# Distance bias made inside the loop over x and moved to GpSimd's queue, first half's final norm among the second half's products, result stored by partition

## The chip, the cores and the metric

The kernel runs on one core of one Trainium2 chip. The metric is the device time of one execution in microseconds (us). Before the change it is 2591.85 us, the median of three runs (2590.37 to 2592.15).

A core has engines that each work through their own list of instructions in order: PE (TensorE, matrix products, results into eight PSUM banks of 128 x 512 f32), DVE (VectorE) and ACT (ScalarE) for elementwise work, POOL (GpSimd) and SP (SyncE). Transfers between the chip's memory (HBM) and the on-chip memory (SBUF) are issued here by SP and by POOL; each of the two feeds a queue of its own, and 16 DMA engines carry out both.

## The reference, cut to what matters

One decoder layer on 512 tokens of width 2048:

```python
u = rmsnorm(h, norm_mix_g)
qa, ka, va, qb, kb, vb, g_low, ob_gate, gate_a, gate_b = split(u @ w_in)
ya = sliding_window_attention(qa, ka, va, sinks, rel_bias) @ w_proj_a
yb = (rmsnorm(gated_linear_attention(qb, kb, vb, log_a)) * silu(ob_gate)) @ w_proj_b
h = h + (sigmoid(gate_a) * ya + sigmoid(gate_b) * yb) @ w_out
z = rmsnorm(h, norm_ffn_g)
h = h + (silu(z @ w_ffn_gate) * (z @ w_ffn_up)) @ w_ffn_down
return rmsnorm(h, norm_final_g)
```

In the attention (16 heads, 4 key heads, window 128) a score gets a bias that depends on the head and on the distance between query and key alone, looked up in `rel_bias` (32 buckets x 16 heads), and minus 1e30 outside the window.

## The kernel before, in words

Everything is laid out transposed: features on the 128 partitions, the 512 tokens along the free axis, so the 2048 features are 16 tiles (k or m, `KD` = 16). Each f32 operand is split into a high and a low part in the matmul's own format (`split`, L201: ACT casts the high part, DVE subtracts for the low part), and a product is three matmuls (`mm3`, L238, lines 240 to 242). Weights come in pieces of 128 x 1024 f32, 512 KB. `load_piece` (L212) issues the load of a piece on SP's queue at L219 and splits it; there are three buffers each for the raw piece, its high part and its low part, so SP issues the load of a piece only when the piece three places earlier has been split. `next_piece` (L226) loads ahead by two and also calls up to two closures from a list `side`, which holds work to be put among the products.

Outside of one block that is ordered by hand (the FFN), a planner orders each engine's instructions: by the place in the program where an instruction could run, by readiness in the planner's own reckoning otherwise. Each engine then keeps the planned order and waits where reality is later.

The first stage is the loop over x, L308 to L334: for each of the 16 tiles of x, `fetch` (L298) loads a tile and half a piece of the key and value weights, four tiles ahead. ACT and DVE make `uh` and `ul`, four PSUM banks collect keys and values (12 matmuls per k), and the squares are summed into `ssq`. Then come the first norm (L339: the sums over partitions by PE, the inverse root as a power on POOL at L264 in `inv_rms`, the spreading over partitions by PE in `across`, L273), and behind it the distance bias, L344 to L366: four small loads (`sink_b`, the one-hot table `oh`, `rbt` and the mask `outm`); one matmul pair that picks for each of 16 heads a row of 383 biases by distance (`ps_rb`, L353); one addition of the mask on DVE (`by_dist`); and one DMA that writes each head's row 128 times to memory (`bias_d`, 16 x 128 x 383 f32, 3064 KB). From there each head's 128 x 256 bias tile is read with a stride of one row less one element, which shifts each partition's row by one: L496, two loads of 256 KB for each of the four head groups, at the head of the loop over groups (L486), before the group's query products (`ps_qa`, four pieces, 96 matmuls). The scores of a group (L418, L419) and their masking with the bias on DVE (L424, `attention_weights`) are put into `side` and so come among the products of the group behind it.

The last stage is the last of the eleven down products, L1232 to L1260. It is done in two halves of 256 tokens. For each half, 16 products (12 matmuls of 256 columns each) are added into `acc` by DVE (L1241), squared by ACT (L1246), and the squares summed by DVE (L1248). Then `token_sums` (four matmuls, L283), `inv_rms` (DVE, then POOL), `across` (two diagonals on DVE, matmuls L273), a copy of the result by ACT (L1256), and six calls of `scale_out` (L1213), which scale 1, 1, 2, 4, 4 and 4 of the 16 tiles, on DVE (L1222) or POOL (L1220), and store them through SP (L1230). The six calls of half 0 are put into `side`, one of them after every odd m of half 1; those of half 1 come at the end. The result lies in memory as tile, partition, token, so a stored row is 256 f32 long, 1 KB.

Of the kernel before, what the change touches and what calls it, by code (L numbers as in the profile page):

```python
# [12 lines left out]
F32 = mybir.dt.float32  # L13
# [3 lines left out]
ALU = mybir.AluOpType  # L17
AX = mybir.AxisListType

P = 128  # L20
D = 2048
T = 512
KD = D // P
NT = T // P
A_HEADS, A_KV, HD = 16, 4, 64
WINDOW = 128
N_BUCKETS, MAX_DISTANCE = 32, 128
# [20 lines left out]
TLEN = 383  # L48
# [4 lines left out]
HALF = T // 2  # L53
# [75 lines left out]
def hybrid_layer(  # L129
# [37 lines left out]
    def slot(name, dtype=F32):  # L167
        return tpool.tile([P, T], dtype, tag="t", name=name)

    def work(name, dtype=F32):  # L170
        return held_by["work"].tile([P, T], dtype, tag="w", name=name)
# [4 lines left out]
    def aux_bank(name):  # L176
        pool = banks_of["aux"]
        return pool.tile([P, T], F32, tag="aux" if pool is psa else "mm", name=name)
# [78 lines left out]
    def inv_rms(ssq, n, name, cols=4):  # L257

        ms = small.tile([P, cols], F32, tag="ms", name=f"ms_{name}")
        nc.vector.tensor_scalar(  # L260
            out=ms, in0=ssq, scalar1=1.0 / n, scalar2=EPS, op0=ALU.mult, op1=ALU.add
        )
        r = small.tile([P, cols], F32, tag="rstd", name=f"rstd_{name}")
        nc.gpsimd.tensor_tensor(out=r, in0=ms, in1=halves[:, :cols], op=ALU.pow)  # L264
        return r
# [12 lines left out]
    def token_sums(sqs, name, cols=4):  # L278

        bank = aux_bank(f"ps_s_{name}")  # L280
        for tt in range(cols):
            for i, sq in enumerate(sqs):
                nc.tensor.matmul(  # L283
                    bank[:, tt : tt + 1],
                    lhsT=sq[:, tt * P : (tt + 1) * P],
                    rhs=ones[:, 0:1],
                    start=(i == 0),
                    stop=(i == len(sqs) - 1),
                )
        return bank[:, 0:cols]  # L290


    uh, ul = [], []
    ssq = slot("ssq")
    kv_banks = [mm_bank("ps_kv_0"), mm_bank("ps_kv_1"), aux_bank("ps_kv_2"), aux_bank("ps_kv_3")]
# [12 lines left out]
    for k in range(KD):  # L308
        if k + 4 < KD:
            fetch(k + 4)  # L310
        xt, wf, part = fetched[k]
        wh, wl = (t[:, part] for t in ahead[k // 2])
        uh.append(slot(f"uh_{k}", F32R))
        ul.append(slot(f"ul_{k}", F32R))
        gcol = g_mix_sb[:, k : k + 1]
        nc.scalar.activation(uh[k], xt, AF.Copy, scale=gcol)
        nc.vector.scalar_tensor_tensor(
            out=ul[k],
            in0=xt,
            scalar=gcol,  # L320
            in1=uh[k].bitcast(F32),
            op0=ALU.mult,
            op1=ALU.subtract,
        )
        split(wh, wl, wf[:, part])
        for m in range(4):
            cols = slice(m * P, (m + 1) * P)
            mm3(kv_banks[m], wh[:, cols], wl[:, cols], uh[k], ul[k], k == 0, k == KD - 1)
        if k == 0:
            nc.scalar.activation(ssq, xt, AF.Square)  # L330
        else:
            sq = work(f"xsq_{k}")
            nc.scalar.activation(sq, xt, AF.Square)
            nc.vector.tensor_tensor(out=ssq, in0=ssq, in1=sq, op=ALU.add)  # L334
    taken[0] = KD // 2
    for i in range(2):
        load_piece(taken[0] + i)
# [1 line left out]
    nc.vector.tensor_copy(rstd1, inv_rms(token_sums([ssq], "mix"), D, "mix"))  # L339
    rb1 = const.tile([P, T], F32, name="rb1")  # L340
    nc.vector.tensor_copy(rb1, across(rstd1, "mix"))


    sink_b = const.tile([P, A_HEADS], F32, name="sink_b")  # L344
    nc.sync.dma_start(sink_b, sinks.to_broadcast([P, A_HEADS]))
    oh = work("oh")
    nc.sync.dma_start(oh[0:N_BUCKETS, 0:TLEN], onehot)
    rbt = small.tile([N_BUCKETS, A_HEADS], F32, tag="rbt", name="rbt", bufs=1)
    nc.sync.dma_start(rbt, rel_bias)
    outm = work("outm")  # L350
    nc.sync.dma_start(outm[0:A_HEADS, 0:TLEN], outside)
    ps_rb = aux_bank("ps_rb")
    nc.tensor.matmul(  # L353
        ps_rb[0:A_HEADS, 0:TLEN], lhsT=rbt, rhs=oh[0:N_BUCKETS, 0:TLEN], start=True, stop=True
    )
    by_dist = work("by_dist")
    nc.vector.tensor_tensor(
        out=by_dist[0:A_HEADS, 0:TLEN],
        in0=ps_rb[0:A_HEADS, 0:TLEN],
        in1=outm[0:A_HEADS, 0:TLEN],  # L360
        op=ALU.add,
    )
    nc.sync.dma_start(
        bias_d,
        by_dist[0:A_HEADS, 0:TLEN].rearrange("h (o t) -> h o t", o=1).to_broadcast([A_HEADS, P, TLEN]),
    )  # L366

    kh, kl = [], []
    for m in range(2):
# [116 lines left out]
    for g in range(A_KV):  # L486
        bias = []
        for hp in range(2):
            b = slot(f"bias_{g}_{hp}").rearrange("p (h k) -> p h k", h=2)
            h0 = 4 * g + 2 * hp  # L490
            src = bass.AP(
                bias_d.tensor,
                bias_d.offset + h0 * P * TLEN + (P - 1),
                [[TLEN - 1, P], [P * TLEN, 2], [1, 2 * P]],
            )
            nc.sync.dma_start(b, src)  # L496
            bias.append(b)
        banks = project(uh, ul, f"qa{g}")
        qs = []
        for m in range(2):  # L500
            qf = slot(f"qf_{g}_{m}")
            nc.vector.tensor_tensor(out=qf, in0=banks[m], in1=rb1, op=ALU.mult)
            for half in range(2):
                rows = slice(half * HD, (half + 1) * HD)
                other = slice((1 - half) * HD, (2 - half) * HD)
                q = slot(f"q_{g}_{m}_{half}", F32R)
                nc.scalar.activation(q[rows], qf[rows], AF.Copy, scale=HD**-0.5)
                nc.vector.scalar_tensor_tensor(
                    out=q[other],
                    in0=qf[rows],  # L510
                    scalar=HD**-0.5,
                    in1=q[rows].bitcast(F32),
                    op0=ALU.mult,
                    op1=ALU.subtract,
                )
                qs.append(q)
        for n in range(NT):
            side.append(partial(attention_weights, g, n, qs, bias, held))
            if n:
                side.append(partial(attention_values, g, n - 1, held))  # L520
        side.append(partial(attention_values, g, NT - 1, held))
# [691 lines left out]
    def scale_out(m0, n, tag, cols, bank, rb):  # L1213

        out = wpool.tile([P, 4, HALF], F32, tag=tag, name=f"out_{cols.start}_{m0}")
        for i in range(n):
            m = m0 + i
            a = acc[m][:, cols]
            if by_gpsimd(m):
                nc.gpsimd.tensor_tensor(out=out[:, i], in0=a, in1=rb, op=ALU.mult)  # L1220
            else:
                nc.vector.scalar_tensor_tensor(  # L1222
                    out=out[:, i],
                    in0=a,
                    scalar=g_final_sb[:, m : m + 1],
                    in1=bank,
                    op0=ALU.mult,
                    op1=ALU.mult,
                )
        nc.sync.dma_start(outT[m0 : m0 + n, :, cols].rearrange("m p t -> p m t"), out[:, 0:n])  # L1230

    for half in range(2):  # L1232
        cols = slice(half * HALF, (half + 1) * HALF)
        sums = work(f"osum_{half}")[:, 0:HALF]
        for m in range(KD):
            wh, wl = wd[m]
            bank = mm_bank(f"ps_fd_{half}_{m}")[:, 0:HALF]
            for j in range(4):
                mm3(bank, wh[:, j], wl[:, j], fh[j][:, cols], fl[j][:, cols], j == 0, j == 3)
            a = acc[m][:, cols]  # L1240
            nc.vector.tensor_tensor(out=a, in0=bank, in1=a, op=ALU.add)  # L1241
            if m == 0:
                nc.scalar.activation(sums, a, AF.Square)
            else:
                s2 = work(f"osq_{half}_{m}")[:, 0:HALF]
                nc.scalar.activation(s2, a, AF.Square)  # L1246
            if 0 < m < KD - 1:
                nc.vector.tensor_tensor(out=sums, in0=sums, in1=s2, op=ALU.add)  # L1248
            if by_gpsimd(m):
                nc.scalar.activation(a, a, AF.Copy, scale=g_final_sb[:, m : m + 1])  # L1250
            if m % 2 == 1 and side:
                side.pop(0)()
        r = inv_rms(token_sums([sums, s2], f"fin{half}", 2), D, f"fin{half}", 2)
        bank = across(r, f"fin{half}", 2)[:, 0:HALF]
        rb3 = slot(f"rb3_{half}")[:, 0:HALF]
        nc.scalar.copy(rb3, bank)  # L1256
        m0 = 0
        for n, tag in zip((1, 1, 2, 4, 4, 4), ("wf", "wh", "wl") * 2):
            side.append(partial(scale_out, m0, n, tag, cols, bank, rb3))
            m0 += n  # L1260
    while side:
        side.pop(0)()

# [49 lines left out]
```

## Time and profile before

| | |
|---|---|
| median of 3 runs | 2591.85 us |
| the profiled execution | 2590.59 us, of which the span from the first to the last instruction or transfer is 2588.8 us |
| PE busy | 2545.2 us, 98% of the span |
| DVE, ACT, POOL busy | 1501.4, 1005.9 and 159.4 us |
| DMA | 415.05 MB, 160 GB/s over the span |
| queue of SP, of POOL | 371.15 MB (45.6% of the DMA engines' span), 41.95 MB (10.6%) |

In the rows below, a row of a timeline has start, duration, engine, line, operation, the tile written and those read, and the shapes. Matmuls are pipelined, and each is shown until its modelled end, so that rows overlap; the pace is read from the starts. "Waits" names who ended an idle time, with the sum, the number and the longest.

### The profile page before, as it was taken

To read this page: it belongs to the slowest core of one execution; us is meant where nothing else is said; L and a number is where in the kernel's file an instruction comes from. 1 tells how busy PE (TensorE), PEld (TensorE's weight loads), DVE (VectorE), ACT (ScalarE), POOL (GpSimd) and SP (SyncE) were. 2 spreads that over 40 slices of the span, in tenths; PEclk is the share of its full clock that TensorE was granted. 3 is DMA by queue.
4 is the path that set the end of the run, shared out by engine and by line. 5 is a ranking of instruction groups with operands and counts; after the bars stand their busy time and mean duration, and the time that the engine had idled before them with its cause. 6 is when DMAs were issued, how large, how long until landed. Compare 5 with 4: busy or idle time off the path is not lost.

```text
span 2588.8 us, 30598 instructions
## 1 busy us (share of the span) xinstructions
PE 2545.2 (98%) x11678; PEld 2109.2 (81%) x11678; DVE 1501.4 (58%) x2209; ACT 1005.9 (39%) x1436; POOL 159.4 (6%) x202
## 2 busy tenths in 40 slices
PE   8999999999999999999899999999999999999997
PEld 7777888888888888888688888888888888888886
DVE  6695463643333334446975766666666657575755
ACT  5464332322222223223444444444344444444443
POOL 0000000000000000000001011110111010101011
PEclk9999999999999999999999999999999999999998
DMA  6622223234333332544578787777878787878782
GB/s 197 130 80 65 90 74 98 74 122 128 124 123 110 96 97 65 197 144 144 198 208 207 209 202 221 198 213 187 234 186 225 198 219 203 213 204 209 207 216 101
DMA packets 151730, 415.05 MB, mean 160 GB/s; under 512 B 15888, under 2 KB 24256, under 8 KB 151584
## 3 DMA queue, kind: packets, MB, share of 16 engines
q1 hardware_dynamic: 128544, 371.15, 45.6%
q0 software_dynamic: 23040, 41.95, 10.6%
q8 instruction: 91, 1.49, 0.2%
q14 instruction: 55, 0.45, 0.1%
HBM read 355.38 MB, written 57.66 MB: 160 GB/s over the span
## 4 chain that ended last, share of the span: by engine, by line
PE 82%; issue 11%; DVE 5%; DMA 1%; ACT 1%; POOL 0%; SPq 0%; DVEq 0%; ACTq 0%; POOLq 0%
PE ps_ua L970 8%; PE ps_fd L241 6%; PE ps_fd L242 6%; PE ps_fd L240 6%; PE ps_ue L970 5%; PE ps_uf L970 5%; PE ps_ub L970 4%; PE ps_ud L970 4%; PE ps_uc L970 4%; PE ps_ga L240 2%; PE ps_ga L241 2%; PE ps_gb L240 2%; PE ps_gb L241 2%; PE ps_ga L242 2%; PE ps_gb L242 2%
## 5 line engine op out<-in xcount | busy, mean ns | idle before, releaser
L1168 DVE TENSOR_TENSOR tl<-wq,th 128x1024 fp32r<-128x1024 f32 x420 | 511.2, 1221 | 457.3 <-ACT th L1165 455.0
L1165 ACT CAST th<-wq 128x1024 fp32r<-128x1024 f32 x420 | 441.5, 1052 | 457.9 <-PE ps_ua L970 116.5
L204 DVE TENSOR_TENSOR wl<-wf,wh 128x1024 fp32r<-128x1024 f32 (+1 forms) x176 | 206.3, 1173 | 378.5 <-ACT wh L203 369.9
L203 ACT CAST wh<-wf 128x1024 fp32r<-128x1024 f32 (+1 forms) x176 | 177.9, 1012 | 536.4 <-PE ps_ga L241 115.7
L240 PE MATMUL ps_fd<-fh,th 128*128 128x512 f32 x640 | 249.1, 389 | 0.0
L241 PE MATMUL ps_fd<-fl,th 128*128 128x512 f32 x640 | 249.0, 389 | 0.0
L242 PE MATMUL ps_fd<-fh,tl 128*128 128x512 f32 x640 | 249.0, 389 | 0.0
L1116 POOL DMA_DIRECT2D h_d<-fd x160 | 138.3, 864 | 1154.1 <-ACT fd L1115 1148.4
L1115 ACT COPY fd<-ps_fd 128x512 f32<-128x512 f32 x160 | 93.9, 587 | 289.3 <-PE ps_fd L242 286.7
L240 PEld LDWEIGHTS ps_fd<-fh,th 128*128 128x128 f32 x640 | 120.1, 188 | 25.0
L241 PEld LDWEIGHTS ps_fd<-fl,th 128*128 128x128 f32 x640 | 120.1, 188 | 24.9
L242 PEld LDWEIGHTS ps_fd<-fh,tl 128*128 128x128 f32 x640 | 120.1, 188 | 24.9
L970 PE MATMUL ps_ue<-th,zs 128*128 128x512 f32 x352 | 123.7, 392 | 2.2 <-DVE c L1032 2.2
L240 PE MATMUL ps_wo<-mgh,th 128*128 128x512 f32 x256 | 99.8, 390 | 1.5 <-DVE sgb L805 1.2
L242 PE MATMUL ps_wo<-mgh,tl 128*128 128x512 f32 x256 | 99.7, 389 | 0.5 <-DVE tl L1168 0.5
L240 PE MATMUL ps_ga<-uh,wh 128*128 128x512 f32 x256 | 100.1, 391 | 0.0
L242 PE MATMUL ps_ga<-uh,wl 128*128 128x512 f32 x256 | 99.6, 389 | 0.0
L241 PE MATMUL ps_ga<-ul,wh 128*128 128x512 f32 x256 | 99.6, 389 | 0.0
L241 PE MATMUL ps_wo<-mgl,th 128*128 128x512 f32 x256 | 99.6, 389 | 0.0
L240 PE MATMUL ps_gb<-uh,wh 128*128 128x512 f32 x256 | 99.6, 389 | 0.0
L242 PE MATMUL ps_gb<-uh,wl 128*128 128x512 f32 x256 | 99.6, 389 | 0.0
L241 PE MATMUL ps_gb<-ul,wh 128*128 128x512 f32 x256 | 99.6, 389 | 0.0
(614 smaller groups left out, 5597.9 us busy)
## 6 DMA issues: line engine op xcount, KB each, us to landing
wq<-in_quads_dram SPq DMA_DIRECT2D x352, 512.0 KB, 4.7
wf<-in_pieces_dram SPq DMA_DIRECT2D x160, 512.0 KB, 3.6
wq<-in_pieces_dram SPq DMA_DIRECT2D x112, 512.0 KB, 4.5
h_d<-fd POOLq DMA_DIRECT2D x160, 256.0 KB, 5.4
x<-in_xT_dram SPq DMA_DIRECT2D x16, 256.0 KB, 4.9
wf<-in_pieces_dram SPq DMA_DIRECT2D x16, 256.0 KB, 4.7
mA_d<-sga SPq DMA_DIRECT2D x16, 256.0 KB, 3.0
ya<-mA_d SPq DMA_DIRECT2D x16, 256.0 KB, 3.0
```

The lines of the kernel that those rows point to most:

```text
L203: nc.scalar.copy(dst_hi, src)
L204: nc.vector.tensor_tensor(out=dst_lo, in0=src, in1=dst_hi.bitcast(F32), op=ALU.subtract)
L240: nc.tensor.matmul(ps, lhsT=ah, rhs=bh, start=first, stop=False)
L241: nc.tensor.matmul(ps, lhsT=ah, rhs=bl, start=False, stop=False)
L242: nc.tensor.matmul(ps, lhsT=al, rhs=bh, start=False, stop=last)
L970: nc.tensor.matmul(ps, lhsT=a, rhs=b, start=first and n == 0, stop=last and n == 2, skip_group_check=True)
L1115: nc.scalar.copy(part, bank)
L1116: nc.gpsimd.dma_start(h_d[m], part, accum_op=ALU.add)
L1165: nc.scalar.copy(hi, src)
L1168: tt(out=lo, in0=src, in1=hi.bitcast(F32), op=ALU.subtract)
```

## The change

Three edits. The four loads of the bias tables move to the front of the loop over x and to POOL's queue; the matmul pair, the addition and the write of `bias_d` become a function that is called after the tile k = 8 of the loop, with the write on POOL's queue, and the eight loads of `bias` go to POOL's queue too. In the last stage, the norm of half 0 goes into `side`, in two steps with an empty step before each, and `side` is served after every m instead of every odd one; half 1's norm stays where it was. The result is laid out in memory as half, partition, tile, token, so that the tiles of one store lie side by side in a row; the host puts them back in order.

```diff
+    sink_b = const.tile([P, A_HEADS], F32, name="sink_b")
+    nc.gpsimd.dma_start(sink_b, sinks.to_broadcast([P, A_HEADS]))
+    oh = work("oh")
+    nc.gpsimd.dma_start(oh[0:N_BUCKETS, 0:TLEN], onehot)
+    rbt = small.tile([N_BUCKETS, A_HEADS], F32, tag="rbt", name="rbt", bufs=1)
+    nc.gpsimd.dma_start(rbt, rel_bias)
+    outm = work("outm")
+    nc.gpsimd.dma_start(outm[0:A_HEADS, 0:TLEN], outside)
+
+    def lay_out_bias():
+        ps_rb = aux_bank("ps_rb")
+        nc.tensor.matmul(
+            ps_rb[0:A_HEADS, 0:TLEN], lhsT=rbt, rhs=oh[0:N_BUCKETS, 0:TLEN], start=True, stop=True
+        )
+        by_dist = work("by_dist")
...
+        nc.gpsimd.dma_start(
+            bias_d,
+            by_dist[0:A_HEADS, 0:TLEN].rearrange("h (o t) -> h o t", o=1).to_broadcast([A_HEADS, P, TLEN]),
+        )
@@ in the loop over x @@
+        if k == KD // 2:
+            lay_out_bias()
@@ after the first norm: the same lines taken out, with nc.sync @@
...
-            nc.sync.dma_start(b, src)
+            nc.gpsimd.dma_start(b, src)
@@ last stage @@
-        nc.sync.dma_start(outT[m0 : m0 + n, :, cols].rearrange("m p t -> p m t"), out[:, 0:n])
+        nc.sync.dma_start(outT[cols.start // HALF, :, m0 : m0 + n], out[:, 0:n])
+    fin = {}
+    def fin_sums(half, sums, s2):
+        fin[half] = inv_rms(token_sums([sums, s2], f"fin{half}", 2), D, f"fin{half}", 2)
+    def fin_scale(half, cols):
+        bank = across(fin[half], f"fin{half}", 2)[:, 0:HALF]
+        rb3 = slot(f"rb3_{half}")[:, 0:HALF]
+        nc.scalar.copy(rb3, bank)
+        m0 = 0
+        for n, tag in zip((1, 1, 2, 4, 4, 4), ("wf", "wh", "wl") * 2):
+            side.append(partial(scale_out, m0, n, tag, cols, bank, rb3))
+            m0 += n
...
-            if m % 2 == 1 and side:
+            if side:
                 side.pop(0)()
...
+        last_norm = [partial(fin_sums, half, sums, s2), partial(fin_scale, half, cols)]
+        if half == 0:
+            side += [lambda: None, last_norm[0], lambda: None, last_norm[1]]
+        else:
+            for f in last_norm:
+                f()
@@ kernel() @@
-    args.append(nc.dram_tensor("out_0_dram", (KD, P, T), F32, kind="ExternalOutput").ap())
+    args.append(nc.dram_tensor("out_0_dram", (2, P, KD, HALF), F32, kind="ExternalOutput").ap())
```

## Rows read from the trace of the kernel before

**Rows 1.** The page, the chain that ended last, shares of the span by engine.

```profile
PE 82%; issue 11%; DVE 5%; DMA 1%; ACT 1%; POOL 0%; SPq 0%; DVEq 0%; ACTq 0%; POOLq 0%
```

**Rows 2.** Waits of PE, first 130 us: who waited for whom, us in total, times, longest.

```profile
PE ps_kv L240 <- ACT wh L203: 5.8, 1, 5.8
PE ps_qa L240 <- ACT wh L203: 4.4, 1, 4.4
...
PE ps_qa L242 <- DVE wl L204: 0.2, 1, 0.2
```

**Rows 3.** The chain that ended last, 60 to 105 us: start, us, what.

```profile
64.07 29.15 DMA wf<-in_pieces_dram
93.32 1.05 ACT wh L203
```

**Rows 4.** DMA issues from 56 to 92 us: count, size of each, median us from issue to landing.

```profile
bias_d<-by_dist SPq DMA_DIRECT2D x1, 3064.0 KB, 35.4
wf<-in_pieces_dram SPq DMA_DIRECT2D x2, 512.0 KB, 27.6
```

**Rows 5.** The same from 33 to 56 us.

```profile
wf<-in_pieces_dram SPq DMA_DIRECT2D x5, 512.0 KB, 3.5
```

**Rows 6.** Waits of SP's queue, first 130 us.

```profile
SPq L496 <- DMA bias_d<-by_dist: 20.4, 1, 20.4
```

**Rows 7.** Windows: stretch and length, busy us and number of instructions of PE, its weight loads, DVE, ACT and POOL; granted clock, share of the DMA engines, GB/s.

```profile
33.00:56.00 23.00, 22.16 (x102) 17.65 (x101) 7.90 (x15) 4.30 (x5) 1.03 (x1) 1.00 0.31 94
56.00:92.00 36.00, 33.24 (x152) 26.99 (x150) 15.31 (x26) 10.14 (x19) 0.00 (x0) 1.00 0.89 120
92.00:96.00 4.00, 1.33 (x4) 0.77 (x4) 1.57 (x2) 2.63 (x4) 0.00 (x0) 0.90 0.89 290
96.00:103.00 7.00, 7.00 (x26) 5.81 (x26) 6.76 (x16) 2.92 (x4) 0.00 (x0) 0.57 0.83 269
```

**Rows 8.** Timeline of PE around the change of halves and at the end of half 1.

```profile
2541.94 0.28 PE L242 MATMUL ps_fd<-fh,wld 128*128 128x256 f32 x1
2546.29 0.59 PE L283 MATMUL ps_s_fin<-ones,osum 128*128 128x1 f32 x2 [4.08 <-DVE osum L1248]
...
2550.75 0.56 PE L240 MATMUL ps_fd<-fh,whd 128*128 128x256 f32 x1
...
2552.82 0.29 PE L240 MATMUL ps_fd<-fh,whd 128*128 128x256 f32 x1
...
2553.06 0.28 PE L242 MATMUL ps_fd<-fh,wld 128*128 128x256 f32 x1
...
2574.66 0.28 PE L242 MATMUL ps_fd<-fh,wld 128*128 128x256 f32 x1
```

**Rows 9.** Timeline of PE from the end of the loop over x to the second group's query products.

```profile
51.38 0.94 PE L283 MATMUL ps_s_mix<-ones,ssq 128*128 128x1 f32 x8
...
54.85 0.81 PE L353 MATMUL ps_rb<-oh,rbt 32*16 32x383 f32 x2
...
89.14 0.39 PE L240 MATMUL ps_qa<-uh,wh 128*128 128x512 f32 x1
...
89.59 0.39 PE L242 MATMUL ps_qa<-uh,wl 128*128 128x512 f32 x1
94.42 0.50 PE L240 MATMUL ps_qa<-uh,wh 128*128 128x512 f32 x1 [4.44 <-ACT wh L203]
...
98.70 0.63 PE L240 MATMUL ps_qa<-uh,wh 128*128 128x512 f32 x1
99.12 0.63 PE L241 MATMUL ps_qa<-ul,wh 128*128 128x512 f32 x1
...
102.33 0.28 PE L418 MATMUL ps_s<-kh,q 128*128 128x256 f32 x1
```

**Rows 10.** Groups of POOL's instructions over the whole span: busy us, mean ns of one, idle before.

```profile
L1116 POOL DMA_DIRECT2D h_d<-fd x160 | 138.3, 864 | 1154.1 <-ACT fd L1115 1148.4 <-issue 3.8 <-DMA wq<-in_quads_dram 1.9
```

**Rows 11.** Timelines of POOL, DVE and SP's queue in the first 100 us.

```profile
52.61 1.03 POOL L264 TENSOR_TENSOR rstd_mix<-ms_mix,halves 128x4 f32<-128x4 f32 x1 [50.11 <-DVE ms_mix L260]
...
76.54 0.68 DVE L502 TENSOR_TENSOR qf<-ps_qa,rb 128x512 f32<-128x512 f32 x1
...
37.00 6.13 SPq L219 DMA_DIRECT2D wf<-in_pieces_dram  x2
```

**Rows 12.** DMA issues from 1000 to 2400 us.

```profile
wq<-in_quads_dram SPq DMA_DIRECT2D x329, 512.0 KB, 4.7
...
h_d<-fd POOLq DMA_DIRECT2D x144, 256.0 KB, 5.4
```

**Rows 13.** Timeline of ACT at the change of halves: the last square of half 0.

```profile
2546.60 0.42 ACT L1246 ACTIVATE osq<-acc 128x256 f32<-128x256 f32 x1 [0.82 <-DVE acc L1241]
```

**Rows 14.** Groups of instructions from 2551 to 2575 us: busy us, mean ns, idle before.

```profile
L1241 DVE TENSOR_TENSOR acc<-ps_fd,acc 128x256 f32<-128x256 f32 x16 | 6.8, 423 | 2.9 <-PE ps_fd L242 1.8
L1248 DVE TENSOR_TENSOR osum<-osum,osq 128x256 f32<-128x256 f32 x14 | 5.9, 423 | 4.5 <-ACT osq L1246 4.5
...
L1222 DVE SCALAR_TENSOR_TENSOR out<-acc,g_final_sb,ps_b_fin 128x256 f32<-128x256 f32 x11 | 4.7, 473 | 1.5 <-ACT rb L1256 1.5
```

**Rows 15.** Windows of the last microseconds, columns as in rows 7.

```profile
2583.00:2584.00 1.00, 0.00 (x0) 0.00 (x0) 0.64 (x2) 0.00 (x0) 0.00 (x0) 0.50 1.02 338
```

**Rows 16.** DMA traffic from 10 to 31 us in 40 slices, GB/s.

```profile
GB/s 402 410 406 398 390 382 398 378 382 394 382 398 378 386 390 382 398 378 386 371 191 51 242 172 382 355 398 297 164 187 242 336 230 125 272 129 169 187 296 303
```

**Rows 17.** The twelve stores of the result (the tile `out_dram`).

```profile
DMA to landing us min/median/max: 1.7/2.6/4.1
```

**Rows 18.** The chain that ended last, 2535 to 2590 us.

```profile
2575.91 0.84 PE ps_s_fin L283 x6
...
2578.08 0.73 PE ps_b_fin L273 x4
```

More of the change, by code (lines that the diff above doesn't have):

```diff
@@ L290, in token_sums @@
         return bank[:, 0:cols]
+    sink_b = const.tile([P, A_HEADS], F32, name="sink_b")
[12 more added lines that the diff above has]
+        by_dist = work("by_dist")
+        nc.vector.tensor_tensor(
+            out=by_dist[0:A_HEADS, 0:TLEN],
+            in0=ps_rb[0:A_HEADS, 0:TLEN],
+            in1=outm[0:A_HEADS, 0:TLEN],
+            op=ALU.add,
+        )
+        nc.gpsimd.dma_start(
+            bias_d,
+            by_dist[0:A_HEADS, 0:TLEN].rearrange("h (o t) -> h o t", o=1).to_broadcast([A_HEADS, P, TLEN]),
+        )
     uh, ul = [], []
@@ L341, in hybrid_layer @@
     nc.vector.tensor_copy(rb1, across(rstd1, "mix"))
[L344 to L366, printed above, removed]
     kh, kl = [], []
@@ L1250, in hybrid_layer @@
                 nc.scalar.activation(a, a, AF.Copy, scale=g_final_sb[:, m : m + 1])
-            if m % 2 == 1 and side:
+            if side:
                 side.pop(0)()
[L1253 to L1260, printed above, removed]
+        last_norm = [
+            partial(fin_sums, half, sums, s2),
+            partial(fin_scale, half, cols),
+        ]
+        if half == 0:
[3 more added lines that the diff above has]
+                f()
     while side:
@@ L1311 @@
     r = run_bass_kernel_spmd(nc, [arrays], core_ids=[0])
-    return np.ascontiguousarray(r.results[0]["out_0_dram"].reshape(D, T).T).reshape(1, T, D)
+    out = r.results[0]["out_0_dram"].reshape(2, P, KD, HALF)
+    return np.ascontiguousarray(out.transpose(0, 3, 2, 1)).reshape(1, T, D)
```

## The prediction

> **What bounds the kernel.** I read the page first, then the two stretches that the diff touches. TensorE makes up 82% of the chain that ended last [rows 1]; so an edit is worth only the time in which PE stands still or runs slowly because of it. The table of waits of the first 130 us has one such place after the start-up: a query product waits 4.4 us for the cast of a weight piece [rows 2]. The chain of waits says why: that piece was asked for at 64.07 us and its DMA took 29.15 us [rows 3]. The list of DMA issues shows what stood before it: `bias_d`, 3064 KB, 35.4 us from issue to landing, on the same queue, SP's [rows 4]; issued at 56.36 us it lands at about 91.8 us, and the piece lands just after it, though half a megabyte lands in 3.5 us in the stretch before [rows 5]. SP itself then waits 20.4 us for the same write before it can issue the first load from it [rows 6]. The windows give the rest of the price: the granted clock is 1.00 until 92 us, 0.90 and then 0.57 in the stretch after PE's wait [rows 7]. At the other end, the timeline of PE shows no product between 2541.94 and 2550.75 us: between the halves of the last product it waits for the sums of squares of half 0, for the inverse root and for its spreading over the partitions, and starts again slowly [rows 8].
>
> **Bias, what the old place costs.** A 512-column matmul follows the one before by 0.225 us at full clock (89.14 to 89.59, two steps) and by 0.42 us at the lower level, 1.2 instead of 2.4 GHz (98.70 to 99.12) [rows 9]. The product that would have begun at 89.82 begins at 94.42: 4.6 us. From 94.42 to 102.3, when the score products again go at full rate, the engine does about half the work: 7.9 us x (1 - 0.225/0.42) = 3.7 us. With 0.2 us of waiting for the low part [rows 2], 8.5 us in all; more than this the bias edit cannot give.
>
> **Bias, the new place.** Moved are one pair of fp32 matmuls, one addition on DVE, four small DMAs and the write; they leave SP for POOL's queue, as do the eight loads of `bias`. Nothing in number changes on PE: the pair costs its 0.8 us [rows 9] wherever it is. It comes after the products of k = 8. The loop over x ends at 51.38 [rows 9]; seven more k of 12 products are 7 x 12 x 0.227 = 19.1 us, so the pair runs at about 32.3, the addition is done by 33.2 and POOL issues the write by 33.8 (estimates). POOL's issue of a DMA of 128 rows takes 0.86 us [rows 10]; this one has 16 x 128 = 2048 rows, so between 0.9 and 16 x 0.86 = 14 us. Even 14 us end at 48, ahead of POOL's next duty, the inverse root at 52.61 [rows 11], so it costs nothing. Two work buffers are held from the start to k = 8; DVE and ACT lead PE there, and PE waits for neither after its first product [rows 2], which I price at 0, between 0 and 0.5 us.
>
> The write then has the DMA engines nearly to itself: they are 0.31 busy from 33 to 56 us and 0.89 under the write [rows 7]. If it keeps its pace, it lands at 33.8 + 35.4 = 69.2. If its share and the pieces' add up on serial engines, it takes 0.9 x 35.4 / (1 - 0.31) = 46 us, to 80. A load of `bias` follows in about 1.7 us of issue (256 rows) and 4 us to landing: 75 to 86 for the first, 1.7 us more for the second. Who needs it? `qf` of the first group is formed at 76.54 [rows 11], so the first masked score could run at about 79 and those of the second pair of heads at 81.5. Late by anything between nothing and 8 us, then; in the middle of the bounds (write down at 75, loads at 80.5 and 82) by about 1 to 2 us. What is queued behind a late score on DVE is the low part of the next piece, and PE has a piece and more ready (a piece is 24 products, 5.4 us), so I charge 1.0 us of the 8.5 and take **7.5 us**; the ends are 8.5 and, with the whole wait back, 0.
>
> Does another queue free the weights? The trace has both queues at work in the long middle stretch: POOL's `h_d` transfers land in 5.4 us, and SP's pieces in 4.7 beside them [rows 12], against 3.5 with SP alone [rows 5]. That is sharing, not standing in line; and the piece of 64.07 is needed at 89.82, so a landing time of 10 or even 20 us stays hidden. The Trainium skill says the contrary of a plain reading of this edit: in "DMA: Bandwidth & Descriptors", section "Issuing engines are not separate DMA queues", DMAs started by different engines run on the same 16 DMA engines, and starting them from several saves only the sequencer's time. The same page, section "Queues, rings and completion order", has each DMA engine go round-robin over its rings, which rows 12 bear out so far; taken alone, the first would leave the pieces behind the write, the fourth case below.
>
> **The norm of half 0.** Before, half 1 starts at 2550.75 instead of 2542.06: 8.7 us, of which the four sums and four spreading products, 0.84 and 0.73 us where they come a second time at the end [rows 18], stay with some 1.7 us. Then nine matmuls from 2550.75 to 2552.82 take 2.07 us, at 0.12 us each (the pace after it) they would take 1.1: 1.0 us. At most 8.7 - 1.7 + 1.0 = 8.0 us are to be had. Now two products of half 1 (m = 0, 1) go first, then the sums, two more, then the spreading, and the six scalings at m = 4 to 9. A product is 12 matmuls of 0.12 = 1.44 us. PE comes to the sums at 2542.06 + 2.88 = 2544.94; but DVE runs behind PE at this point, and the last square of half 0 is ready at 2546.60 + 0.42 = 2547.02 [rows 13]. So PE waits there about 2.1 us, where it waited 4.1 before. The sums end at 2547.8; 14 products, 20.2 us, and the spreading, 0.7 us, end at 2568.7. The last product of half 1 began its last matmul at 2574.66 before [rows 8], so ended its issue at 2574.8: **6.1 us** gained. The inverse root and the diagonals (1.9 us after the sums) are hidden by m = 2 and 3, 2.9 us. What must still fit is DVE: in the 24 us of half 1 it has 16 additions into `acc`, 14 into the sum and 11 scalings, 6.8 + 5.9 + 4.7 = 17.4 us as listed, and 4.5 us of waiting for ACT's squares [rows 14]; that now has 21.7 us, and scalings put into those waits make it fit narrowly. Ends: 8.0, if the planner puts the sums later, and 3, if the clock falls again (1 us) and DVE ends 2 us late.
>
> **The store.** With rows of 1 KB the last 2 MB leave at 338 GB/s with the DMA engines fully busy [rows 15]; x and the first pieces, in rows of 2 KB, came in at 371 to 410 GB/s, most often about 390 [rows 16]. A group of four now has rows of 4 KB, 128 instead of 512. 2.1 MB / 338 = 6.2 us against 5.4 at 390: 0.8 us; if the slowest landing, 4.1 us, becomes the median of all stores, 2.6 [rows 17], it is 1.5. I take **0.7**, near the first, between 0 and 1.5; below nothing I exclude, since the same bytes go in fewer packets.
>
> **Sum.** 7.5 + 6.1 + 0.7 = 14.3 us. The profiled execution took 2590.59 us (span 2588.8): 2576.3. The median of the runs shown is 1.26 us above it, so as a median 2577.5 us.
>
> **Rivals.** (1) *The bias comes late.* The write is stretched to 46 us or more; scores and everything behind them on DVE wait 5 to 8 us, PE follows, and the clock falls as at 92 us. For it: the 0.89 share under the write; against: PE's stock of split pieces. The bias edit gives 0 to 3: 2591.85 - 6.8 - 1.5 = 2583.5. (2) *The half-0 norm hardly moves*, because PE's order has the sums where DVE's lag ends or the scalings crowd DVE, so that it trails: 2 instead of 6.1 us, 2581.6. (3) *Slower: the inverse root behind the load.* POOL takes its work in order. The first load of `bias` now stands on it and waits for the write; the inverse root of the first norm is on POOL too [rows 11]. If the planner lays the load ahead, PE has a few query products to go on with and then stands until the write lands, 69 to 80, instead of 53.7: 16 to 27 us and 3.7 of low clock, against which 8.5 + 6.8 stand. That is slower by 4 to 15, about 2601 us. It decides at one point: whether the planner takes the write to last less than 52.6 - 33.8 = 18.8 us. Against it: the write measured 35.4, and the inverse root stands earlier in the program. (4) *The pieces wait for the write even from another queue.* Then the piece asked for at 37.00 [rows 11], after the write's 33.8, lands behind it at 69.2 + 1.3 = 70.5 and is cast by 71.6; PE needs it four pieces (21.8 us) and some 1.9 us of transposes before 89.82, at about 66.2, and loses 5.4 + 3.7 us, one more than now: 2591.85 - 6.8 + 0.6 = 2585.7.
>
> **Chances.** Forecast 0.60 (its own range 2574 to 2580), (1) 0.18, (2) 0.10, (3) 0.07, (4) 0.05. A difference of 0.2%, 5.2 us, is what can be told from no change; every case but (3) and the poor end of (1), (2) and (4) passes it. Faster 0.84, same 0.08, slower 0.08. The best of all the bounds is 8.5 + 8.0 + 1.5 = 18.0 us: 2573.9, and 1.5 more for a run as low as the lowest shown; upward the range takes in (1) and (2) and (4): 2572.5 to 2587.
>
> **What will show it.** Right: the piece asked for at about 64 us lands within 6 us; the wait of 4.4 us and the clock of 0.57 are gone; `bias_d` is issued by POOL near 34 and lands between 69 and 80; between the halves PE waits about 2 us; the last store lands within 3.5 us. Wrong: PE standing near 54 us for the first norm's diagonal (case 3), DVE waiting for `bias` past 82 us with PE behind it (1), a piece landing only with the write (4), or DVE ending several us after the last product (2).

## The result, and the profile after

The changed kernel takes 2598.94 us (median of 9 runs, 2597.33 to 2600.19) against 2591.32 us of the kernel before beside it: a ratio of 1.0029 (95% interval 1.0019 to 1.0040). It is 7.6 us slower where 14.3 us faster was forecast, and lies outside the range given. The span of its profiled execution is 2596.2 us, 7.4 more than before.

Five marks in the timelines of the two kernels cut the span into stretches, and say where the 7.4 us come from: the start of the first product (L240), of the first norm's sums (L283, the end of the loop over x), of ACT's first cast of `whd` (the weights of the last stage), of the last matmul of the last product, and the end of the span.

| us | until the first product | the loop | to the last stage | last stage to its last matmul | the rest | span |
|---|---|---|---|---|---|---|
| before | 5.8 | 45.6 | 2465.0 | 58.3 | 14.1 | 2588.8 |
| after | 16.7 | 46.8 | 2464.9 | 53.7 | 14.1 | 2596.2 |
| difference | +10.9 | +1.3 | -0.1 | -4.6 | -0.1 | +7.4 |

The loop is longer in part because the matmul pair of the bias now runs in it (0.74 us at 43.69). So the norm of half 0 paid most of what it promised; the bias edit, for which 7.5 us were forecast in the third column, gave nothing there; and 10.9 us were lost before PE had done anything, at a place that the prediction priced at zero.

**The start.** The waits of PE in the first 130 us of the changed kernel (who waited for whom, us in total, times, longest; [rows 2] before):

```profile
PE ps_kv L240 <- ACT uh L343: 16.7, 1, 16.7
PE ps_b_mix L273 <- DVE diag_mix L272: 3.5, 2, 3.4
PE ps_qa L240 <- DVE kf L375: 1.6, 1, 1.6
PE ps_qa L242 <- DVE wl L204: 1.1, 2, 0.5
```

The 4.4 us on the weight piece are gone, as forecast. The first row is the new loss: before, the wait for the first data was 5.8 us long. SP's queue in the first 14 us of the changed kernel says why:

```profile
1.19 10.21 SPq L330 DMA_DIRECT2D wf<-in_pieces_dram  x11
11.44 2.92 SPq L329 DMA_DIRECT2D x<-in_xT_dram  x6
```

The kernel before issues x and weights by turns, the first tile of x at 1.20 us. Here eleven half pieces go first, and the first tile of x is asked for at 11.44. ACT, with its casts done, then waits 5.6 us for that tile, makes `uh` at 15.93, and PE begins at 16.70.

**The first norm.** DVE's timeline around it, and ACT's:

```profile
64.52 0.16 DVE L260 TENSOR_SCALAR ms_mix<-ps_s_mix 128x4 f32<-128x4 f32 x1 [4.14 <-PE ps_s_mix L283]
75.52 1.23 DVE L204 TENSOR_TENSOR wl<-wf,wh 128x1024 fp32r<-128x1024 f32 x1 [10.83 <-ACT wh L203]
81.97 3.75 DVE L204 TENSOR_TENSOR wl<-wf,wh 128x1024 fp32r<-128x1024 f32 x3 [5.22 <-ACT wh L203]
90.23 1.22 DVE L204 TENSOR_TENSOR wl<-wf,wh 128x1024 fp32r<-128x1024 f32 x1 [4.51 <-ACT wh L203]
91.38 0.16 DVE L368 COPY rstd<-rstd_mix 128x4 f32<-128x4 f32 x1
```

```profile
74.44 1.05 ACT L203 CAST wh<-wf 128x1024 fp32r<-128x1024 f32 x1 [15.31 <-DMA wf<-in_pieces_dram]
80.88 1.05 ACT L203 CAST wh<-wf 128x1024 fp32r<-128x1024 f32 x1 [5.39 <-DMA wf<-in_pieces_dram]
```

The input of the inverse root is ready at 64.7, and POOL has formed the root at 65.8 (its row starts at 64.77 and lasts 1.03). Its copy on DVE runs at 91.38, because in DVE's planned order the low parts of five pieces stand ahead of it, and these pieces come late. Four of them were asked for while the write was under way; the fifth was asked for only at 83.22, since its load needs a buffer that a late piece still held. PE itself waits no more than 1.1 us for weights here: what stops it is the copy, which stands on DVE behind the late low parts. The DMA view from 51 to 82 us (queues with packets, MB and share of the 16 engines' time, then the loads of pieces as in [rows 4]), and the write itself from the same view of 30 to 100 us:

```profile
q0 software_dynamic: 619, 2.75, 82.2%
q1 hardware_dynamic: 526, 1.94, 15.3%
...
wf<-in_pieces_dram SPq DMA_DIRECT2D x4, 512.0 KB, 21.8
```

```profile
bias_d<-by_dist POOLq DMA_DIRECT2D x1, 3064.0 KB, 35.7
```

q0 is POOL's queue, q1 SP's. The write takes 82% of that time to move 2.75 MB; the pieces get 15%. In packets the two queues are nearly even, 619 to 526: a packet of the write held its engine for some 0.66 us and one of the loads for 0.14 (estimates: 31 us x 16 engines x share, divided by the packets). The write lands in 35.7 us, as in the kernel before [rows 4], and the pieces pay for it. The windows show the price on PE (columns as in [rows 7]):

```profile
88.00:92.00 4.00, 0.62 (x4) 0.20 (x2) 1.73 (x4) 1.04 (x1) 0.00 (x0) 1.00 0.64 255
92.00:100.00 8.00, 6.24 (x19) 4.89 (x20) 5.23 (x10) 2.47 (x4) 0.03 (x1) 0.57 0.20 66
```

It is the same sequence as in [rows 7], a standstill and then a granted clock of 0.57, with another name on the wait.

**The end.** The waits of PE from 2540 us on:

```profile
PE ps_b_fin L273 <- DVE diag_fin L272: 1.4, 1, 1.4
PE ps_s_fin L283 <- DVE osum L1266: 1.2, 1, 1.2
PE ps_s_fin L283 <- ACT osq L1264: 1.0, 2, 0.6
```

and PE's timeline at the sums of half 0, which now come after two products of half 1:

```profile
2557.13 0.28 PE L242 MATMUL ps_fd<-fh,wld 128*128 128x256 f32 x1
2558.59 0.38 PE L283 MATMUL ps_s_fin<-ones,osum 128*128 128x1 f32 x2 [1.18 <-DVE osum L1266]
2559.37 0.38 PE L283 MATMUL ps_s_fin<-ones,osq 128*128 128x1 f32 x2 [0.40 <-ACT osq L1264]
...
2560.06 0.37 PE L240 MATMUL ps_fd<-fh,whd 128*128 128x256 f32 x1
```

In place of the 8.8 us between the halves [rows 8] there are 2.9 us from the last matmul before the sums to the next product, sums included; the spreading comes two products later and takes 0.4. The price is a spell at the lower clock behind the sums, in a window of the changed kernel (columns as in [rows 7]); the run below with the tables on SP, whose clock did not fall there, has 35 matmuls in the same length:

```profile
2560.00:2564.00 4.00, 4.00 (x22) 4.00 (x23) 1.83 (x6) 0.93 (x2) 0.71 (x1) 0.57 0.00 0
```

```profile
2552.80:2556.80 4.00, 4.00 (x35) 4.00 (x35) 2.16 (x7) 1.28 (x4) 0.71 (x1) 1.00 0.01 2
```

The twelve stores land in

```profile
DMA to landing us min/median/max: 1.7/2.4/3.2
```

which answers to [rows 17]: the slowest is 0.9 us sooner.

### The profile page after: what moved, and what is told of

The parts are those of the page before. It is cut to its first block, busy times and chain, and to the rows that moved or that the text cites. A ratio compares the mean times of both kernels' runs of the same rounds, so it can differ in the third digit from the quotient of the medians.

```text
span 2596.2 us, 30606 instructions
## 1 busy us (share of the span) xinstructions
PE 2544.6 (98%) x11678; PEld 2107.2 (81%) x11678; DVE 1502.9 (58%) x2209; ACT 1006.2 (39%) x1436; POOL 168.7 (6%) x215
## 4 chain that ended last, share of the span: by engine, by line
PE 81%; issue 10%; DVE 6%; DMA 2%; ACT 1%; POOL 0%; SPq 0%; DVEq 0%; ACTq 0%; POOLq 0%
PE ps_ua L974 8%; PE ps_fd L240 6%; PE ps_fd L242 6%; PE ps_fd L241 6%; PE ps_uf L974 4%; PE ps_ue L974 4%; PE ps_ub L974 4%; PE ps_ud L974 4%; PE ps_uc L974 4%; PE ps_ga L240 2%; PE ps_ga L242 2%; PE ps_gb L241 2%; PE ps_gb L240 2%; PE ps_ga L241 2%; PE ps_gb L242 2%
## 5 line engine op out<-in xcount | busy, mean ns | idle before, releaser
L240 PE MATMUL ps_fd<-fh,th 128*128 128x512 f32 x640 | 249.1, 389 | 0.0
L240 PEld LDWEIGHTS ps_fd<-fh,th 128*128 128x128 f32 x640 | 120.1, 188 | 24.9
L240 PE MATMUL ps_wo<-mgh,th 128*128 128x512 f32 x256 | 99.8, 390 | 1.4 <-DVE sgb L809 1.2
L240 PE MATMUL ps_ga<-uh,wh 128*128 128x512 f32 x256 | 100.1, 391 | 0.0
L240 PE MATMUL ps_gb<-uh,wh 128*128 128x512 f32 x256 | 99.6, 389 | 0.0
```

Source lines behind the costliest of these rows:

```text
L240: nc.tensor.matmul(ps, lhsT=ah, rhs=bh, start=first, stop=False)
```

## The experiments

Two questions are open. Why is the start late: the two work buffers, or the four small loads on POOL's queue? And why does the query part gain nothing: because the order laid out for DVE has the first norm behind five pieces (theory P, below), or because the pieces do not arrive in time beside this write (theory S)?

**Two buffers of their own.**

```diff
-    oh = work("oh")
+    oh = slot("oh")
...
-    outm = work("outm")
+    outm = slot("outm")
```

> The changed kernel with the table of buckets and the mask in buffers of their own instead of two of the work buffers that x also takes; their loads stay on POOL's queue. Theory A (the 10.9 us at the start come from the planned order: SP's queue has eleven half pieces ahead of the first x tile, because x's buffers are given out behind the mask's, whose load stands on POOL): the first product moves from 16.7 to about 6 us and the time falls by 10.9 to about 2588 us. Theory B (two work buffers fewer for x make the loop late): also about 2588. Theory C (four loads through POOL's queue hold up the first x transfers): the first product stays at 16 to 17 us, 2599 us.

Measured: 2592.89 us, ratio 1.0006 (0.9997 to 1.0015) to the kernel before. SP's order is x and weights by turns again, its first tile issued at 1.19 us. The tiles of x are work buffers too, taken behind `oh` and `outm`; that they were put off by these is the reading that fits, the runs show only that the order comes back. But the first product starts at 12.0, not near 6. ACT, which made `uh` first before the change (at 4.00 us), now has three casts of weights and a square ahead of it in its planned order, and each cast waits for its piece:

```profile
7.13 0.62 ACT L203 CAST wh<-wf 128x512 fp32r<-128x512 f32 x1 [4.91 <-DMA wf<-in_pieces_dram]
8.76 0.62 ACT L203 CAST wh<-wf 128x512 fp32r<-128x512 f32 x1 [1.01 <-DMA wf<-in_pieces_dram]
10.22 0.62 ACT L203 CAST wh<-wf 128x512 fp32r<-128x512 f32 x1 [0.85 <-DMA wf<-in_pieces_dram]
10.75 0.62 ACT L360 ACTIVATE xsq<-x 128x512 f32<-128x512 f32 x1
11.28 0.70 ACT L343 ACTIVATE uh<-x,g_mix_sb 128x512 fp32r<-128x512 f32 x1
```

The buffers are 4.7 of the 10.9 us.

**The four loads on SP instead**, in work buffers as in the changed kernel.

```diff
-    nc.gpsimd.dma_start(sink_b, sinks.to_broadcast([P, A_HEADS]))
+    nc.sync.dma_start(sink_b, sinks.to_broadcast([P, A_HEADS]))
```

and so for `oh`, `rbt` and `outm`.

> The changed kernel with the four small loads at the same early place, in the same work buffers, but on SP's queue. Theory A: SP's order is x and piece by turns again, after four loads of 0.47 us: first product at about 8 us, about 2590 us. Theory B: the two buffers are still missing, the first product stays at about 16.7 us or the loop has holes further on, 2599 us. Theory C: first product at about 8 us, 2590 us. Together with the run before it tells the three apart.

Measured: 2587.38 us, 0.9987 (0.9977 to 0.9996). The first product starts at 7.6; the 1.8 us that are left are as much as the four issues that SP now makes ahead of x, 0.46 us apart. So the two work buffers cost little by themselves: it takes their being held for loads on POOL. Each of the two edits alone puts x back into its place; with both as in the change, the order turns. The query part still loses: its waits are

```profile
PE ps_b_mix L273 <- DVE diag_mix L272: 4.1, 1, 4.1
PE ps_qa L240 <- DVE kf L375: 1.6, 1, 1.6
```

**The store alone**, on the kernel before.

```diff
-        nc.sync.dma_start(outT[m0 : m0 + n, :, cols].rearrange("m p t -> p m t"), out[:, 0:n])
+        nc.sync.dma_start(outT[cols.start // HALF, :, m0 : m0 + n], out[:, 0:n])
```

> The kernel before with the result laid out by partition and nothing else. My prediction had 0.7 us (0 to 1.5). By the changed kernel's end (last issue 2591.7, span end 2596.2: 4.5 us, before 5.1 us) it gains 0.6 us, about 2590.7 us. Rival: the rows of 4 KB gain nothing, within 0.3 us of before.

Measured: 2590.21 us, 0.9998 (0.9989 to 1.0007): no difference that the times can tell. In the trace the landings are 1.7/2.4/3.2 us again, and the stretch behind the last matmul is 13.6 us instead of 14.1.

**The norm of half 0 alone**, on the kernel before: the third part of the change's diff, from `fin = {}` to `last_norm`. (A first kernel for this exchanged another stretch of the program too and leaves part of the layer out; its time is not used.)

> The kernel before with the norm of half 0 among the products of half 1 and nothing else. Theory 1 (the edit works as in the changed kernel's trace, where the stretch from the first load of the last down piece to the end of the last product got 4.7 us shorter): 2586 to 2587, against 2591; the wait of PE between the halves is under 2 us. Rival (the 4.7 us are only a smaller backlog left behind by the late start): 2590 to 2591. My prediction's term was 6.1 us: 2585.

Measured: 2585.17 us, 0.9978 (0.9969 to 0.9986): 5.75 us, against 6.1 forecast. The wait between the halves, 4.1 us before, is

```profile
PE ps_s_fin L283 <- DVE osum L1262: 1.1, 1, 1.1
```

**The write on ACT's queue**, the tables on SP.

```diff
-        nc.gpsimd.dma_start(
+        nc.scalar.dma_start(
             bias_d,
```

> The changed kernel with the four tables loaded by SP (as in the run with 2587.4) and the write of the bias issued by ACT instead of POOL, at the same place, from the same 16 partitions. Theory P (the query part gained nothing because the order laid out for DVE and POOL puts the inverse root and its copy behind five pieces, as if POOL were busy for as long as the write lasts): the copy of the inverse root comes about 5 us after the loop, the waits of 4.1 and 1.6 us of PE are gone, and the time is 2579 to 2583. Theory S (the pieces starve because the write shares the DMA engines with them, whatever the order): pieces still take about 22 us, PE waits as much for weights as it waited for the diagonals, and the time stays at 2586 to 2588. A third possibility, ACT held for several us by the issue: PE waits for uh inside the loop over x near 35 us.

Measured: 2589.31 us, 0.9993 (0.9985 to 1.0002). DVE's order is now the one that theory P wants, and the copy of the inverse root runs at 57.30, 2 us after the sums. It does not help:

```profile
57.30 0.17 DVE L368 COPY rstd<-rstd_mix 128x4 f32<-128x4 f32 x1 [1.15 <-POOL rstd_mix L264]
57.50 0.48 DVE L272 TENSOR_SCALAR diag_mix<-ident,rstd 128x128 f32<-128x128 f32 x2
63.91 1.23 DVE L204 TENSOR_TENSOR wl<-wf,wh 128x1024 fp32r<-128x1024 f32 x1 [5.92 <-ACT wh L203]
65.05 0.48 DVE L272 TENSOR_SCALAR diag_mix<-ident,rstd 128x128 f32<-128x128 f32 x2
```

Two diagonals are made, then the low part of the next piece is due, and that piece was in flight beside the write until 62.8. PE waits 5.7 us for the third diagonal, and the granted clock of 60 to 70 us is 0.73. The waits of PE show it too:

```profile
PE ps_b_mix L273 <- DVE diag_mix L272: 6.5, 2, 5.7
```

This order, two diagonals, a low part, two diagonals, is also that of the kernel before, where the wait is 0.8 us, with the piece in time. So P falls as the sole cause: with the copy moved up, the loss stays, and the late piece holds up what now stands behind it.

**The queue alone**, on the kernel before: the write and the eight loads on POOL's queue, at the old place behind the norm.

```diff
-    nc.sync.dma_start(
+    nc.gpsimd.dma_start(
         bias_d,
...
-            nc.sync.dma_start(b, src)
+            nc.gpsimd.dma_start(b, src)
```

> The kernel before with the write of the bias and its eight loads on POOL's queue, at the old place behind the first norm. Theory P (sharing costs little, the planned order was the fault): the inverse root stands ahead of the write here, so the order is not disturbed; the pieces take 20 to 26 us beside the write but arrive ahead of need; the wait of 4.4 us and the clock of 0.57 go: 2583 to 2586. Theory S (pieces starve beside the write): the piece wait stays at 2 to 5 us: 2588 to 2592.

Measured: 2590.99 us, 0.9998 (0.9989 to 1.0007). The 4.4 us on `wh` are gone and 4.1 us on `qf` stand in their place. The chain that ended last passes through it (start, us, what):

```profile
69.39 23.72 DMA wf<-in_pieces_dram
...
94.29 1.24 DVE wl L204
...
95.55 6.93 DMA wf<-in_pieces_dram
...
103.65 1.23 DVE wl L204
104.88 0.61 DVE qf L502
```

```profile
PE ps_qa L240 <- DVE qf L502: 4.1, 1, 4.1
```

A piece takes 23.7 us, the next one starts late for it, and `qf` stands behind their low parts on DVE. The queue by itself is worth nothing: with SP alone the pieces stand behind the write, with two queues they crawl beside it, and PE stands still for about as long, some 11 us later.

**The same write from 128 partitions**, on the kernel before, on SP's queue at the old place. Each head's row is made on eight partitions by the same matmul pair (`rbt8` is `rbt` with each column eight times, one small copy on DVE; the mask is loaded to all partitions), and each partition writes 16 copies instead of 128.

```diff
-        bias_d,
-        by_dist[0:A_HEADS, 0:TLEN].rearrange("h (o t) -> h o t", o=1).to_broadcast([A_HEADS, P, TLEN]),
+        bias_d.rearrange("h (j o) t -> (h j) o t", j=8),
+        by_dist[:, 0:TLEN].rearrange("h (o t) -> h o t", o=1).to_broadcast([P, P // 8, TLEN]),
```

> The kernel before with the same 3064 KB written from 128 partitions (each head's row made eight times, each copy written 16 times) instead of from 16 partitions, on SP's queue at the old place. Theory W (the 35 us come of all bytes leaving 16 partitions): at the 338 GB/s of the store of the result the write takes 9 to 12 us, the pieces behind it arrive in time, and the full 8.5 us come back: 2581 to 2584. Rival (the rows of 1.5 KB or the memory side set the 35 us): the write takes 30 us or more, and the time is 2589 to 2592.

Measured: 2586.96 us, 0.9984 (0.9975 to 0.9993). The DMA issues from 56 to 92 us, which answer to [rows 4]:

```profile
bias_d<-by_dist SPq DMA_DIRECT2D x1, 3064.0 KB, 16.6
wf<-in_pieces_dram SPq DMA_DIRECT2D x5, 512.0 KB, 3.6
```

Same bytes, same row length, same queue: 16.6 us instead of 35.4, so most of the write's time went with its leaving 16 partitions; why 16 are slow, the runs do not show. It is not the 9 to 12 us of the expectation. The wait of 4.4 us is gone and the granted clock is 1.00 in every window up to 130 us. The gain is 4.0 us in the times and 4.9 in the stretch to the last stage, not 8.5.

**The wide write at the new place.** The changed kernel with the wide write, on POOL's queue after k = 8, the tables on SP in buffers of their own.

```diff
-    nc.gpsimd.dma_start(outm[0:A_HEADS, 0:TLEN], outside)
+    nc.sync.dma_start(outm[:, 0:TLEN], outside[0:1, :].to_broadcast([P, TLEN]))
```

and the two edits above.

> The changed kernel with the four tables loaded by SP into buffers of their own and the write made from 128 partitions, still issued by POOL after the tile k = 8. Theory S (the query part gained nothing because each piece takes 20 us and more beside the 35 us write): the write takes about 17 us and is over before the loop ends, pieces take 4 to 6 us, PE waits no more than 1 us for the first norm, the last query product of the four groups ends 5 us earlier after the loop than before (127 to 129 us instead of 132.6), and with the tail's 5.7 us and a start later by 1.8 us at most the time is 2580 to 2583. Theory P (POOL is reckoned busy with a write whoever carries it): PE waits 4 us for the diagonals again, 2586 to 2588. If the two work buffers made the start 1.8 us late, the first product begins at 5.8 to 6.2; if the four loads ahead of x did, at 7.6.

Measured: 2585.53 us, 0.9976 (0.9966 to 0.9985). In the query part the signs of theory S came, with the write in 15.9 us and no wait of PE above 1.1 us:

```profile
bias_d<-by_dist POOLq DMA_DIRECT2D x1, 3064.0 KB, 15.9
```

```profile
PE ps_b_mix L273 <- DVE diag_mix L272: 1.1, 1, 1.1
```

Around the first norm DVE's order is that of the run with the write on ACT (the copy at 59.73, 2.3 us after the sums), so the two differ there by how late the piece is: 1.1 us of waiting against 5.7. The changed kernel's own order, the copy behind five pieces, was not run with the fast write; so how much of its loss that order would cause by itself is open. The end of the loop to the last query product is 129.6 us, near the 127 to 129 expected. The time misses the 2580 to 2583 expected, because of the start, which missed both expectations: the first product begins at 10.2 us, since the first tile of x comes behind the mask, which now is 191.5 KB in place of 23.9.

```profile
ACT uh L348 <- DMA x<-in_xT_dram: 6.2, 1, 6.2
```

So this run does not tell whether the 1.8 us belonged to the buffers or to the issues.

**What is left: wide write at the old place, norm of half 0, store.** None of the bias is moved.

> The kernel before with the wide write at the old place on SP's queue, the norm of half 0 among the products of half 1, and the result stored by partition. If the three gains add (4.0 and 5.8 us measured alone, and 0.8 of the trace of the store): 2591 - 10.6 = 2580.4, so 2579 to 2582. If they overlap, since PE comes to the end earlier with DVE as late as before: 2583 to 2585.

Measured: 2580.82 us (2579.56 to 2581.53), 0.9961 (0.9949 to 0.9974) of the kernel before: 10.4 us faster than before and 18 faster than the change. The gains add.

The stretches of all of them, worked out as in the first table:

| us | first product | loop | to the last stage | last stage | rest |
|---|---|---|---|---|---|
| own buffers, tables on POOL | 12.0 | 47.4 | 2465.4 | 53.2 | 14.1 |
| tables on SP | 7.6 | 46.9 | 2467.5 | 51.4 | 13.9 |
| store alone | 5.8 | 45.3 | 2465.1 | 59.6 | 13.6 |
| norm of half 0 alone | 6.3 | 46.2 | 2464.0 | 52.9 | 14.7 |
| write on ACT | 7.8 | 47.3 | 2466.9 | 53.3 | 13.3 |
| queue alone | 5.7 | 46.3 | 2464.0 | 59.1 | 14.7 |
| wide, old place | 5.7 | 45.4 | 2460.1 | 59.2 | 14.6 |
| wide, new place | 10.2 | 47.2 | 2459.4 | 53.5 | 13.3 |
| wide, old place, norm, store | 5.9 | 46.5 | 2460.4 | 53.0 | 13.9 |

The third column falls into two groups: 2464 to 2467.5 with the narrow write, wherever and by whomever it is issued, and 2459.4 to 2460.4 with the wide one.

## Why the prediction was wrong, point by point

**"Two work buffers are held from the start to k = 8 ... which I price at 0, between 0 and 0.5 us"**: this step failed. Without its 10.9 us the change would have been 3.3 us faster; with no other error, 14.3 less 10.9 would still have been 3.4 us faster: the sign is lost by this step and the next together. It looked for the cost in the loop, where DVE and ACT lead PE, and not at the start, where nobody leads. Cost in the trace: 10.9 us. Shown: own buffers, or SP for the loads, each put x back among the weights (first product at 12.0 and 7.6 us instead of 16.7). The four loads moved past the first tile of x, and the prediction never asked what they pass there.

**"A landing time of 10 or even 20 us stays hidden", and with it the term of 7.5 us**: failed. The argument weighed one piece against one due time. What counts is the rate. From 59.1 us, where ACT ended the cast before, to 80.9 it could cast one piece (its row of 74.44, with 15.31 us of waiting for DMA), while PE uses a piece in 5.4 us. The stock just about bridged that for PE, which waited 1.1 us for low parts; it did not for DVE, which works in its planned order: each late low part holds up whatever stands behind it, the copy of the inverse root in the changed kernel, a diagonal with the write on ACT, `qf` with the queue alone. The prediction had only the reverse in view, a low part behind a late score. The row that warned was among the windows: a DMA share of 0.89 for 120 GB/s under the write, beside 0.89 for 290 GB/s in the window after it [rows 7]. A transfer that fills the engines at less than half of their rate is the thing to mend, whatever queue it is on. That the write at the new place would have "the DMA engines nearly to itself" was the second half of the same error; the write did not slow down (issued at 45.31 us, where 33.8 was worked out without the late start, it lasts 35.7), the pieces did: expected within 6 us, they took 21.8, the median of four.

The wait that the prediction removed did go, and the next one took its place. Rival (4) has the place (pieces late because of the write, even from another queue) but not the way: they are not held until the write lands, they get 15.3% of the engines' time beside it. Rival (3) foresaw a standstill of PE at the first norm's diagonal; the inverse root was not late on POOL, though, but its copy on DVE, behind the low parts of pieces, and moving that copy up did not help by itself. The prediction weighed a sentence of the Trainium skill ("DMA: Bandwidth & Descriptors", section "Issuing engines are not separate DMA queues"): starting transfers from several engines saves only the sequencer's time. The queue-alone run agrees, 0.9998. The prediction let it count only through rival (4), at 0.05.

**The upper bound of 8.5 us for the bias.** With the wide write the third stretch is 4.5 us shorter (the mean of the three wide runs, 2460.0, against 2464.5 for the four with the narrow write at the old place, the kernel before among them). The wait of 4.4 us and the lower clock are both gone in those runs, so some 4 us of the bound came back as something else. Part is listed: PE's waits from 52 to 340 us fall from 7.6 to 3.9 us, not by 4.6, since short waits for `ph` and `q` grow. The rest stays open.

**The norm of half 0, 6.1 us**: right in its mechanism, with one term left out. Alone it measured 5.75 us; in the table the last stage is 59.1 us on average without it and 53.0 with it. PE waited 1.6 us for the sums where 2.1 were estimated. In the changed kernel it gave 4.6 us: behind the sums the granted clock is 0.57 for 4 us, in which PE did 13 matmuls fewer than in the run whose clock stayed at 1.00, some 1.6 us at 0.12 us each (an estimate from the two windows above). The forecast had that lower clock only in its lower end, at 1 us. That run, with the tables on SP, has the shortest last stage, 51.4 us. Why the clock fell in one and not in the other the runs do not show; PE waited 1.6 and 1.4 us for the sums there.

**The store, 0.7 us**: right in size as far as the trace can say (the rest averages 14.5 us without the edit and 13.7 with it, 0.8), too small for the times to show.

**POOL's issue of the write, 0.9 to 14 us**: 1.05 us, near the lower end.

## What to carry to other kernels

A transfer that takes the DMA engines' time at a fraction of their rate is not made harmless by another queue or an earlier start, as long as loads are needed beside it; read its GB/s against its share, and spread it over more partitions first. A load moved to the front of a program competes with the first data, where each microsecond counts in full: price the start apart from the steady loop, buffers and planned orders included. And a wait that is removed is worth only what the next late thing leaves: weigh rates (pieces per microsecond against use), not one due time.

## What the runs showed of the hardware

- The same write is faster from more partitions: 3064 KB in rows of 1.5 KB took 35.0 to 36.6 us from 16 partitions, by SP, ACT or POOL, and 15.9 to 16.7 us from 128.
- Two queues do not share the engines' time evenly when one has such a write: in the changed kernel 82.2% went to it and 15.3% to loads of 512 KB, though their packets were 619 and 526. The loads landed after 15.7 to 21.8 us (medians of three kernels: write on ACT, queue alone, the change) instead of 3.5.
- The issue of one DMA of 2048 rows took POOL 1.04 to 1.27 us, ACT 0.64 and SP 0.68 us; one of 128 rows took POOL 0.86 [rows 10]. It doesn't grow in proportion to the rows, as the prediction's upper bound had it.
- Small loads at the start landed later from POOL's queue beside SP's loads of weights, 5.3 and 5.7 us for `oh` and `outm`, than from SP's queue ahead of all of x and the weights, 2.3 and 1.7 us. The runs do not tell the queue from the company.
